# A hybrid decoder layer on one core: where the low parts of the operands are made, how the softmax sum and the head norm's root are formed, and how Strassen's input blocks are split

## The chip, the core and the metric

The kernel runs on one core of one Trainium2 chip. The core has TensorE (PE, matrix products; its weight loads are shown as PEld), VectorE (DVE), ScalarE (ACT), GpSimd (POOL) and the queues that start DMA transfers (SP, and the ACT queue). The metric is the device time of one execution in microseconds (us); lower is better. Times of several runs are given as their median.

## The reference, cut to what matters

One inference step of one layer (DEPTH = 1, D_MODEL = 1024). 2048 prompt tokens with 16 meta tokens in front, and 8 running sequences of 8 tokens each (64 sample tokens), go through

```
z = x @ w_in                                   # q, k, v, c, vm, o, gates
att = swa_attend(q, k, v)                      # 8 heads of 64, 2 KV heads, 128-token band, sinks, ALiBi
  p = exp(s - mx); p = p / (sum(p) + exp(sink - mx)); att = p @ v
h_m = mlstm_chunk(...)                         # 4 heads of 128, causal conv, gates, chunkwise form
y = concat([head_norm(att, g_attn), head_norm(sigmoid(o) * h_m, g_mlstm)])
  head_norm(h, g) = (h - mean) * rsqrt(var + 1e-5) * g          # per head
x1 = layer_norm(ALPHA * x + y @ w_out)
ffn = (silu(x1 @ w_gate) * (x1 @ w_up)) @ w_down                # d_ff = 2816
out = layer_norm(ALPHA * x1 + ffn)
```

All inputs and outputs are fp32. The attention's v is centred over each head before it is used, so the mean of `att` over a head is zero and its variance is the mean square.

## The kernel before

**Products.** Most products use operands in a reduced form of fp32 (`F32R`). Each fp32 operand is split into a high part (a cast, done by `hi_of`, on ACT nearly always) and a low part (source minus high part, `split`, line 144, on the engine `veng`). `mm3` (lines 147 to 149) then issues three matmuls: high x high, high x low, low x high.

**Stages.** (1) Projection of v, gates and o for all tokens in 17 tiles. (2) Projection of q, k and the conv path in five groups of 426 tokens; while it runs, chunks of attention and mLSTM are worked off in the background. (3) The FFN stage, in four groups of tokens (widths `W2` = 512, 512, 544, 544). Each group has an output projection (`out_proj`), the first layer norm (`ln1`), gate and up products by Strassen's scheme with seven products (`strassen`, P1 to P7, inputs B11, B21, B22 and the differences T1 to T4, each half a group wide), the down projection (`down`) and the second layer norm (`ln2`).

**Weights.** Each weight block (128 x 512) is loaded by the SP queue into `wr`, and `wblock` splits it: high part on ACT (line 135), low part on DVE, or on POOL where the block's number modulo 5 is 1 or 3 (`NPW`), two of five. Blocks are made `LOOK` = 5 ahead of their use. `sums` makes the sums of weights for Strassen's scheme on POOL early on and stores them in `SW`.

**Background.** `bg_attn(c)` is one 128-query chunk of attention and `bg_ml(c)` one of mLSTM; both are generators that are advanced one step at a time between the products (`pace`), and drained (`bg_drain`) where a group needs them. In `bg_attn`, the scores go to `P` (line 567), ACT takes the exponentials with their sums in `den` (line 575), DVE scales each head's `P` by 1/`den` (line 581), TensorE transposes (line 591) and multiplies by v (line 598). Then `att_rstd` (lines 516 to 531) forms the head norm: squares on ACT, split in two, a product with a constant block matrix `blk` that gives every element the mean square of its head (128 x 512), and on that whole width `rsqrt`: an integer start value and three Newton steps, nine wide operations (lines 158 to 160) behind lines 527, 153 and 155. The layer norms use a compact form, `spread_rstd`: per-token sums by matmuls with one column (line 499), the root on a few columns, and matmuls with the identity that spread it over the partitions again (line 511).

**Second layer norm.** `ln2` of a group runs as a generator `pend`, advanced in `after` behind the products P3 and P5 of the next group; while it is pending, the background is not advanced. Its squares are summed on POOL and DVE (line 1159).

**Order.** The functions are written out in the order of the products, but each engine's queue is ordered by a planner at build time, which simulates the kernel by estimated durations; a tile that waits for a free buffer waits in that order. The pools that matter here: `xpl` with 22 tiles (`x_tile`, for Y, the split input blocks and the first projection), `fp` with 7 `ft` tiles (`ftmp`), 6 `xx` tiles for the input blocks used last, 16 `z` tiles.

Of the kernel before, what the change touches and what calls it, by code (L numbers as in the profile page):

```python
# [17 lines left out]
KD = 8  # L18
# [33 lines left out]
NPW = (1, 3)  # L52
# [10 lines left out]
def tile_hymba(  # L63
# [47 lines left out]
    blk = cp.tile([128, 128], F32R, name="blk")  # L111
# [4 lines left out]
    def constants():  # L116
        SP.dma_start(out=C, in_=cst)
        SP.dma_start(out=Q, in_=par)
        SP.dma_start(out=R, in_=rows.to_broadcast([128, 16]))
        V.memset(avg, 1.0 / D)  # L120
        V.memset(one1, 1.0)
        V.tensor_copy(blk, C[:, C_BD:C_BD + 128])
# [393 lines left out]
    def att_rstd(o, w):  # L516

        sq = t2k("pt", [128, 512], PTB)
        A.activation(out=sq[:, 0:w], in_=o[:, 0:w], func=AF.Square)
        sh, sl = (t2k("pt", [128, 512], PTB, F32R) for _ in range(2))  # L520
        split("a", sh[:, 0:w], sl[:, 0:w], sq[:, 0:w])
        yield
        var = bps()
        PE.matmul(var[:, 0:w], lhsT=blk, rhs=sh[:, 0:w], start=True, stop=False)
        PE.matmul(var[:, 0:w], lhsT=blk, rhs=sl[:, 0:w], start=False, stop=True)
        ve = t2k("pt", [128, 512], PTB)
        V.tensor_scalar(out=ve[:, 0:w], in0=var[:, 0:w], scalar1=EPS, scalar2=None, op0=ALU.add)
        ry, tt = (t2k("pt", [128, 512], PTB) for _ in range(2))
        rsqrt(ve[:, 0:w], ry[:, 0:w], tt[:, 0:w])
        yield  # L530
        return ry

    def bg_attn(c):
# [45 lines left out]
        V.reciprocal(out=den, in_=den)  # L579
        for h in range(8):  # L580
            V.tensor_scalar(out=Pt[:, h, 0:nk], in0=Pt[:, h, 0:nk], scalar1=den[:, h:h + 1],
                            scalar2=None, op0=ALU.mult)
# [26 lines left out]
        rb = yield from att_rstd(o, 512)  # L609
# [129 lines left out]
    def bg_sample_attn():  # L739
# [64 lines left out]
        rb = yield from att_rstd(o, 256)  # L804
# [251 lines left out]
    with ExitStack() as s2:  # L1056
# [113 lines left out]
        def ln1(g, fast=False, marks={}):  # L1170


            z, w = P[g]["z"], WH[g]
            x = P[g]["x"] = {}
            for b in ("B11", "B21", "T2", "T1", "T3", "B22", "T4"):
                x[b] = []
                for k in range(4):
                    own = b == "T4" or b == "B22" and k > 1
                    x[b].append(fp.tile([128, FW], F32R, tag="xx", name="x", bufs=6) if own else x_tile())

            def hl(b, k, src, veng=V):
                t = x[b][k]
                return split("a", t[:, 0:w], t[:, HW:HW + w], src, veng)
# [8 lines left out]
            a, b = slice(0, w), slice(w, 2 * w)  # L1192
# [9 lines left out]
            t1, t2 = [], []  # L1202
            for k in range(4):
                t = ftmp()
                t1.append(t[:, 0:w])
                t2.append(t[:, HW:HW + w])
                G.tensor_tensor(out=t1[k], in0=z[k][:, b], in1=z[k][:, a], op=ALU.subtract)
                V.tensor_tensor(out=t2[k], in0=z[k + 4][:, b], in1=t1[k], op=ALU.subtract)
                hl("T2", k, t2[k])
                hl("T1", k, t1[k])  # L1210
                if k % 2:
                    yield
            for k in range(4):
                t = ftmp()
                t3, t4 = t[:, 0:w], t[:, HW:HW + w]
# [47 lines left out]
        def strassen(S, name):  # L1263
# [5 lines left out]
            def fn(wb):  # L1269
# [8 lines left out]
                x = [(t[:, 0:w], t[:, HW:HW + w]) for t in P[S["g"]]["x"][xs]]  # L1278
                product(p, wb, x, name in ("P1", "P2", "P5"), True, True)
# [16 lines left out]
                after(name)  # L1296
# [5 lines left out]
        def after(name):  # L1302
            if pend[0] is not None:
                if name in ("P3", "P5") and next(pend[0], 0) == 0:
# [76 lines left out]
        for g in range(NG):  # L1381
# [49 lines left out]
            else:  # L1431
# [13 lines left out]
                for m in range(KD):  # L1445
                    down(g, s, m, cc[1:], True, KD - 1, step(gen, 1))
# [129 lines left out]
```

## Time and profile before

| what | value |
|---|---|
| time before, median of 2 runs | 2691.45 us (2690.14 to 2692.76) |
| the profiled execution | 2694.93 us |
| its span, first to last instruction | 2693.1 us |
| mean granted TensorE clock | 0.954 |
| DMA | 409.29 MB, mean 152 GB/s |
| instructions | 44641 |

How to read the rows below: a group row gives line, engine, operation, output<-inputs, shapes and count, then the busy time in us and the mean duration of one in ns, then the idle time of the engine just before it and who ended that. Busy times of one engine can overlap in themselves, TensorE's above all, since its matmuls are pipelined. A waits row reads "who waited <- for whom: us in total, times, longest".

### The profile page before, as it was taken

Reading aid. Unit: us, or ns where it says so; the run is one execution under the profiler, and the core shown is the slowest. Engines: PE = TensorE matmul, PEld = TensorE weight load, DVE = VectorE, ACT = ScalarE, POOL = GpSimd, SP = SyncE. Lnnn points to the kernel's source line nnn. Section 1 sums busy time; section 2 is a strip of 40 time slices with the busy share of each in tenths; the row PEclk is TensorE's granted clock in tenths of the full one; section 3 lists DMA queues with packets and bytes.
Section 4 is the critical chain, followed back from the end, with each engine's and each line's share of the span. In section 5 each row is a group of like instructions: output and inputs, shape, how many; then the busy total and the mean of one; then the engine's idle time right before and its main releaser. Section 6 shows DMA issues by size and latency. Waiting matters only on the chain. (4 is left out here: it accounts for less than half of the span.)

```text
span 2693.1 us, 44641 instructions
## 1 busy us (share of the span) xinstructions
PE 2447.9 (91%) x16021; PEld 2234.5 (83%) x16021; DVE 1743.9 (65%) x3726; ACT 1183.3 (44%) x2598; POOL 914.7 (34%) x815
## 2 busy tenths in 40 slices
PE   9999889766999999988999989789999998899996
PEld 8999777655887888767888888688889997899996
DVE  5224365667677877677887785865775558755556
ACT  3113333444544555346454452452444535444453
POOL 3323333204322333363332233632222247322234
PEclk9999999868999999988999999799999998999997
DMA  8644766542554545425554553265444532444443
GB/s 295 221 137 162 241 210 220 174 142 80 163 151 151 158 154 156 150 63 190 165 154 142 159 167 99 59 202 145 128 137 142 170 94 88 140 137 141 137 149 105
DMA packets 302713, 409.29 MB, mean 152 GB/s; under 512 B 31442, under 2 KB 172842, under 8 KB 302474
## 3 DMA queue, kind: packets, MB, share of 16 engines
q1 hardware_dynamic: 260240, 351.54, 43.1%
q10 hardware_dynamic: 42250, 54.89, 5.6%
q8 instruction: 126, 2.06, 0.3%
q14 instruction: 97, 0.79, 0.1%
HBM read 339.26 MB, written 68.06 MB: 151 GB/s over the span
## 5 line engine op out<-in xcount | busy, mean ns | idle before, releaser
L147 PE MATMUL gps<-x,w 128*128 128x272 f32 (+3 forms) x2968 | 875.3, 302 | 68.0 <-ACT ft L1288 28.7
L135 ACT CAST w<-wr 128x512 fp32r<-128x512 f32 (+1 forms) x898 | 541.6, 611 | 839.1 <-PE gps L148 725.4
L144 POOL TENSOR_TENSOR w<-wr,w 128x512 fp32r<-128x512 f32 (+1 forms) x360 | 491.1, 1365 | 1200.7 <-ACT w L135 1101.8
L148 PE MATMUL gps<-x,w 128*128 128x272 f32 (+3 forms) x2968 | 879.8, 298 | 20.3 <-DVE x L144 20.2
L149 PE MATMUL gps<-x,w 128*128 128x272 f32 (+3 forms) x2968 | 866.8, 298 | 7.0 <-DVE w L144 5.5
L147 PEld LDWEIGHTS gps<-x,w 128*128 128x128 f32 x2968 | 564.8, 192 | 101.3 <-ACT ft L1288 31.3
L148 PEld LDWEIGHTS gps<-x,w 128*128 128x128 f32 x2968 | 571.4, 193 | 36.4 <-DVE x L144 26.4
L149 PEld LDWEIGHTS gps<-x,w 128*128 128x128 f32 x2968 | 565.7, 193 | 18.2 <-DVE w L144 6.3
L144 DVE TENSOR_TENSOR w<-wr,w 128x512 fp32r<-128x512 f32 (+1 forms) x538 | 423.6, 793 | 160.6 <-ACT w L135 136.7
L147 PE MATMUL gps<-h,w 128*128 128x272 f32 (+1 forms) x1056 | 351.3, 335 | 28.7 <-DVE z L1321 16.9
L148 PE MATMUL gps<-h,w 128*128 128x272 f32 (+1 forms) x1056 | 345.8, 328 | 4.2 <-DVE h L144 4.2
L149 PE MATMUL gps<-h,w 128*128 128x272 f32 (+1 forms) x1056 | 343.7, 327 | 1.0 <-DVE w L144 1.0
L147 PEld LDWEIGHTS gps<-h,w 128*128 128x128 f32 x1056 | 200.9, 191 | 54.9 <-DVE z L1321 25.5
L1321 DVE SCALAR_TENSOR_TENSOR z<-z,gps 128x272 f32<-128x272 f32 (+1 forms) x240 | 122.7, 516 | 149.7 <-PE gps L149 149.3
L148 PEld LDWEIGHTS gps<-h,w 128*128 128x128 f32 x1056 | 201.7, 191 | 19.8 <-DVE h L144 6.0
L149 PEld LDWEIGHTS gps<-h,w 128*128 128x128 f32 x1056 | 201.3, 191 | 18.3 <-DVE w L144 1.4
L198 POOL TENSOR_TENSOR st<-sa 128x256 f32<-128x256 f32 x88 | 67.7, 790 | 215.3 <-DMA SW<-st 180.6
L144 DVE TENSOR_TENSOR x<-x 128x426 fp32r<-128x426 f32 (+3 forms) x72 | 54.5, 757 | 103.1 <-ACT x L135 86.9
L1122 POOL TENSOR_TENSOR zs<-zs,z 128x512 f32<-128x512 f32 (+2 forms) x58 | 76.6, 1323 | 46.9 <-DVE z L1135 30.5
L135 ACT CAST x<-x 128x426 fp32r<-128x426 f32 (+3 forms) x72 | 42.0, 585 | 109.7 <-DMA x<-in_xT 55.5
L1254 DVE SCALAR_TENSOR_TENSOR ft<-ft 128x512 f32<-128x512 f32 (+1 forms) x88 | 76.6, 883 | 12.5 <-ACT ft L1253 12.0
L1257 DVE SCALAR_TENSOR_TENSOR ft<-ft 128x512 f32<-128x512 f32 (+1 forms) x88 | 79.6, 906 | 7.6 <-ACT ft L1294 6.1
(351 smaller groups left out, 3841.1 us busy)
## 6 DMA issues: line engine op xcount, KB each, us to landing
wr<-SW SPq DMA_DIRECT2D x352, 256.0 KB, 2.8
wr<-in_wd SPq DMA_DIRECT2D x168, 256.0 KB, 2.8
wr<-in_wg SPq DMA_DIRECT2D x132, 256.0 KB, 2.8
wr<-in_wu SPq DMA_DIRECT2D x132, 256.0 KB, 2.8
SW<-st ACTq DMA_DIRECT2D x44, 512.0 KB, 5.2
wr<-in_wo SPq DMA_DIRECT2D x64, 256.0 KB, 2.8
sa<-in_wg SPq DMA_DIRECT2D x22, 512.0 KB, 4.7
sa<-in_wu SPq DMA_DIRECT2D x22, 512.0 KB, 4.8
```

The source lines that it names most:

```text
L135: A.copy(out, src)
L144: return veng.tensor_tensor(out=lo, in0=src, in1=hi.bitcast(F32), op=ALU.subtract)
L147: PE.matmul(out, lhsT=wh, rhs=xh, start=start, stop=False, **kw)
L148: PE.matmul(out, lhsT=wh, rhs=xl, start=False, stop=False, **kw)
L149: PE.matmul(out, lhsT=wl, rhs=xh, start=False, stop=stop, **kw)
L198: G.tensor_tensor(out=t[:, i], in0=x, in1=y, op=op)
L1122: G.tensor_tensor(out=s[:, c], in0=s[:, c], in1=z[m][:, c], op=ALU.add)
L1254: V.scalar_tensor_tensor(out=c, in0=t, scalar=1.0, in1=c, op0=ALU.add, op1=ALU.mult)
L1257: V.scalar_tensor_tensor(out=c, in0=c, scalar=0.5, in1=P[g]["gate"].pop(2 * S["q"] + i), op0=ALU.mult, op1=ALU.mult)
L1321: V.scalar_tensor_tensor(out=zm, in0=zm, scalar=ALPHA if s == 0 else 1.0, in1=p, op0=ALU.mult, op1=ALU.add)
```

## The change

1. `NPW` becomes empty: the low part of every weight block is made on DVE.
2. `bg_attn` no longer scales `P` by 1/`den`. The unscaled product goes on, and `att_rstd` gets `den`: since the head norm divides by the root of variance + EPS, the unscaled variance is used with EPS x den x den.
3. `att_rstd` is compact: the squares are not split; four matmuls (two columns each) give the mean square per query and head, the root is taken on 8 columns (4 in the sample chunk), and eight matmuls with the identity spread it. The constant `blk` goes.
4. In `ln1` the differences for T1 and T3 are made on DVE, and the low parts of B22 and T4 too. Blocks are split two at a time into shared tiles: B21 with B22 (directly from z), T1 with T2, T3 with T4; B11 stays alone.
5. `after` advances the pending `ln2` only from the second round of products (q > 0) on.
6. In the last group, the first three of the last eight down items advance `ln2` by two steps, not one.

```diff
-NPW = (1, 3)
+NPW = ()
...
-    def att_rstd(o, w):
+    def att_rstd(o, nb, den=None):
+        w, k = 128 * nb, 2 * nb
         sq = t2k("pt", [128, 512], PTB)
         A.activation(out=sq[:, 0:w], in_=o[:, 0:w], func=AF.Square)
-        sh, sl = (t2k("pt", [128, 512], PTB, F32R) for _ in range(2))
-        split("a", sh[:, 0:w], sl[:, 0:w], sq[:, 0:w])
+        vp = bps()
+        for t in range(nb):
+            PE.matmul(vp[:, 0:k].rearrange("p (g t) -> p t g", g=2)[:, t, :], lhsT=sq[:, 128 * t:128 * t + 128],
+                      rhs=C[:, C_BD:C_BD + 128:64], start=True, stop=True)
+        t_ = t2k("rs", [128, 24], 2)
+        ve, ry, tt = t_[:, 0:k], t_[:, 8:8 + k], t_[:, 16:16 + k]
+        if den is None:
+            V.tensor_scalar(out=ve, in0=vp[:, 0:k], scalar1=EPS, scalar2=None, op0=ALU.add)
+        else:
+            V.scalar_tensor_tensor(out=tt, in0=den, scalar=EPS, in1=den, op0=ALU.mult, op1=ALU.mult)
+            V.tensor_tensor(out=ve, in0=tt, in1=vp[:, 0:k], op=ALU.add)
+        rsqrt(ve, ry, tt)
         yield
-        var = bps()
-        PE.matmul(var[:, 0:w], lhsT=blk, rhs=sh[:, 0:w], start=True, stop=False)
-        PE.matmul(var[:, 0:w], lhsT=blk, rhs=sl[:, 0:w], start=False, stop=True)
-        ve = t2k("pt", [128, 512], PTB)
-        V.tensor_scalar(out=ve[:, 0:w], in0=var[:, 0:w], scalar1=EPS, scalar2=None, op0=ALU.add)
-        ry, tt = (t2k("pt", [128, 512], PTB) for _ in range(2))
-        rsqrt(ve[:, 0:w], ry[:, 0:w], tt[:, 0:w])
-        yield
-        return ry
+        rb = bps()
+        for t in range(nb):
+            for g in range(2):
+                PE.matmul(rb[64 * g:64 * g + 64, 128 * t:128 * t + 128],
+                          lhsT=ry[:, nb * g + t:nb * g + t + 1].to_broadcast([128, 64]), rhs=ident,
+                          start=True, stop=True)
+        return rb
...
         V.tensor_tensor(out=den, in0=den, in1=es, op=ALU.add)
-        V.reciprocal(out=den, in_=den)
-        for h in range(8):
-            V.tensor_scalar(out=Pt[:, h, 0:nk], in0=Pt[:, h, 0:nk], scalar1=den[:, h:h + 1], ...)
...
-            for b in ("B11", "B21", "T2", "T1", "T3", "B22", "T4"):
-                    own = b == "T4" or b == "B22" and k > 1
+            x11 = [x_tile() for _ in range(4)]
+            for n in ("B", "T", "U"):
+                for d in (xh, xl):
+                    d[n] = [own() if n == "U" and (d is xl or k > 1) else x_tile() for k in range(4)]
...
+            def hl2(n, k, src, names, veng=V):
+                h, l = xh[n][k], xl[n][k]
+                for m, c in zip(names, (a, b)):
+                    x[m][k] = (h[:, c], l[:, c])
+                return split("a", h[:, 0:2 * w], l[:, 0:2 * w], src, veng)
...
-                hl("B11", k, z[k][:, a])
-                marks[7] = hl("B21", k, z[k + 4][:, a]).ins
+                hl1(k, z[k][:, a])
+                marks[7] = hl2("B", k, z[k + 4][:, 0:2 * w], ("B21", "B22")).ins
...
-                G.tensor_tensor(out=t1[k], in0=z[k][:, b], in1=z[k][:, a], op=ALU.subtract)
-                V.tensor_tensor(out=t2[k], in0=z[k + 4][:, b], in1=t1[k], op=ALU.subtract)
-                hl("T2", k, t2[k])
-                hl("T1", k, t1[k])
+                V.tensor_tensor(out=t[:, a], in0=z[k][:, b], in1=z[k][:, a], op=ALU.subtract)
+                V.tensor_tensor(out=t[:, b], in0=z[k + 4][:, b], in1=t[:, a], op=ALU.subtract)
+                hl2("T", k, t[:, 0:2 * w], ("T1", "T2"))
...
-                G.tensor_tensor(out=t3, in0=z[k + 4][:, b], in1=z[k][:, b], op=ALU.subtract)
-                V.tensor_tensor(out=t4, in0=z[k + 4][:, a], in1=t2[k], op=ALU.subtract)
-                hl("T3", k, t3)
-                hl("B22", k, z[k + 4][:, b], G)
-                hl("T4", k, t4, G)
+                V.tensor_tensor(out=t[:, a], in0=z[k + 4][:, b], in1=z[k][:, b], op=ALU.subtract)
+                V.tensor_tensor(out=t[:, b], in0=z[k + 4][:, a], in1=ts[k][:, b], op=ALU.subtract)
+                hl2("U", k, t[:, 0:2 * w], ("T3", "T4"))
...
-                if name in ("P3", "P5") and next(pend[0], 0) == 0:
+                if S["q"] and name in ("P3", "P5") and next(pend[0], 0) == 0:
...
-                    down(g, s, m, cc[1:], True, KD - 1, step(gen, 1))
+                    down(g, s, m, cc[1:], True, KD - 1, step(gen, 2 if m < 3 else 1))
```

More of the change, by code (lines that the diff above doesn't have):

```diff
@@ L110, in tile_hymba @@
     avg = cp.tile([128, 128], F32, name="avg")
-    blk = cp.tile([128, 128], F32R, name="blk")
     ident = C[:, C_ID:C_ID + 128]
@@ L121, in constants @@
         V.memset(one1, 1.0)
-        V.tensor_copy(blk, C[:, C_BD:C_BD + 128])
     NC4 = (NCH + 1) * 4
@@ L578, in bg_attn @@
         V.tensor_tensor(out=den, in0=den, in1=es, op=ALU.add)
-        V.reciprocal(out=den, in_=den)
-        for h in range(8):
-            V.tensor_scalar(out=Pt[:, h, 0:nk], in0=Pt[:, h, 0:nk], scalar1=den[:, h:h + 1],
-                            scalar2=None, op0=ALU.mult)
         yield
@@ L608, in bg_attn @@
                          scale=Q[:, Q_GA + t:Q_GA + t + 1])
-        rb = yield from att_rstd(o, 512)
+        rb = yield from att_rstd(o, 4, den)
         ysf = ys.rearrange("p t q -> p (t q)")
@@ L803, in bg_sample_attn @@
                 yield
-        rb = yield from att_rstd(o, 256)
+        rb = yield from att_rstd(o, 2)
         ys = t2k("ys", [128, 4, 128], 2)
@@ L1173, in ln1, with own, hl1 @@
             z, w = P[g]["z"], WH[g]
-            x = P[g]["x"] = {}
-            for b in ("B11", "B21", "T2", "T1", "T3", "B22", "T4"):
-                x[b] = []
-                for k in range(4):
-                    own = b == "T4" or b == "B22" and k > 1
[L1179 to L1183, printed above, removed]
+            a, b = slice(0, w), slice(w, 2 * w)
+            x = P[g]["x"] = {n: [None] * 4 for n in ("B11", "B21", "B22", "T1", "T2", "T3", "T4")}
+            def own():
+                return fp.tile([128, FW], F32R, tag="xx", name="x", bufs=6)
+            x11 = [x_tile() for _ in range(4)]
+            xh, xl = {}, {}
+            for n in ("B", "T", "U"):
+                for d in (xh, xl):
+                    d[n] = [own() if n == "U" and (d is xl or k > 1) else x_tile() for k in range(4)]
+            def hl1(k, src):
+                t = x11[k]
+                x["B11"][k] = (t[:, 0:w], t[:, HW:HW + w])
+                return split("a", t[:, 0:w], t[:, HW:HW + w], src)
+            def hl2(n, k, src, names, veng=V):
[3 more added lines that the diff above has]
+                return split("a", h[:, 0:2 * w], l[:, 0:2 * w], src, veng)
             cc = [slice(o, o + n) for o, n in cols(W2[g])]
@@ L1191, in ln1 @@
                     yield
-            a, b = slice(0, w), slice(w, 2 * w)
             for k in range(4):
@@ L1197, in ln1 @@
                                  bias=Q[:, Q_L1B + kk:Q_L1B + kk + 1])
-                hl("B11", k, z[k][:, a])
-                marks[7] = hl("B21", k, z[k + 4][:, a]).ins
+                hl1(k, z[k][:, a])
+                marks[7] = hl2("B", k, z[k + 4][:, 0:2 * w], ("B21", "B22")).ins
                 if k % 2:
                     yield
-            t1, t2 = [], []
+            ts = []
             for k in range(4):
                 t = ftmp()
-                t1.append(t[:, 0:w])
-                t2.append(t[:, HW:HW + w])
-                G.tensor_tensor(out=t1[k], in0=z[k][:, b], in1=z[k][:, a], op=ALU.subtract)
-                V.tensor_tensor(out=t2[k], in0=z[k + 4][:, b], in1=t1[k], op=ALU.subtract)
-                hl("T2", k, t2[k])
-                hl("T1", k, t1[k])
+                ts.append(t)
+                V.tensor_tensor(out=t[:, a], in0=z[k][:, b], in1=z[k][:, a], op=ALU.subtract)
+                V.tensor_tensor(out=t[:, b], in0=z[k + 4][:, b], in1=t[:, a], op=ALU.subtract)
+                hl2("T", k, t[:, 0:2 * w], ("T1", "T2"))
                 if k % 2:
@@ L1277, in fn @@
                 p = S["be" if name == "P2" else "ga" if name in ("P5", "P3") else "al"][:, a]
-                x = [(t[:, 0:w], t[:, HW:HW + w]) for t in P[S["g"]]["x"][xs]]
-                product(p, wb, x, name in ("P1", "P2", "P5"), True, True)
+                product(p, wb, P[S["g"]]["x"][xs], name in ("P1", "P2", "P5"), True, True)
                 c1, c2 = S["c"]
@@ L1295, in fn, with after @@
                     gated(S, 1)
-                after(name)
+                after(S, name)
             item(fn, (wsrc(S["mt"], S["q"], ws), 4))
         pend, rate = [None], [0.0]
-        def after(name):
+        def after(S, name):
             if pend[0] is not None:
-                if name in ("P3", "P5") and next(pend[0], 0) == 0:
+                if S["q"] and name in ("P3", "P5") and next(pend[0], 0) == 0:
                     pend[0] = None
```

1 line of the change is left out of this document (removed).

## The prediction

> **What bounds the kernel now.** I read the shares of the engines first, then the windows by stage, then TensorE's waits, and last the single operations that stand in those waits. In a windows row the columns are the stretch, its length, then busy time and (count) for PE, PEld, DVE, ACT and POOL, the granted TensorE clock, the DMA share and GB/s.
>
> ```profile
> PE 2447.9 (91%) x16021; PEld 2234.5 (83%) x16021; DVE 1743.9 (65%) x3726; ACT 1183.3 (44%) x2598; POOL 914.7 (34%) x815
> ...
> 505.00:577.00 72.00, 37.48 (x163) 26.35 (x161) 50.90 (x171) 25.53 (x67) 3.27 (x3) 0.71 0.40 119
> 660.00:677.00 17.00, 0.62 (x3) 0.33 (x2) 16.34 (x28) 13.11 (x35) 9.16 (x12) 0.50 0.00 0
> ...
> 700.00:1100.00 400.00, 376.97 (x2617) 336.37 (x2616) 316.70 (x712) 207.06 (x482) 114.36 (x83) 0.99 0.51 156
> 1250.00:1690.00 440.00, 419.58 (x2870) 374.16 (x2870) 334.21 (x714) 215.34 (x495) 135.00 (x100) 0.99 0.51 155
> ...
> 1229.00:1237.00 8.00, 0.43 (x4) 0.22 (x3) 3.75 (x4) 3.48 (x7) 7.76 (x6) 0.65 0.41 131
> 1760.00:1769.00 9.00, 0.69 (x4) 0.51 (x3) 5.83 (x5) 5.02 (x10) 8.74 (x6) 0.72 0.41 127
> 2287.00:2293.00 6.00, 1.50 (x12) 1.28 (x11) 4.74 (x5) 2.80 (x7) 5.76 (x6) 1.00 0.61 182
> 2360.00:2400.00 40.00, 40.00 (x322) 40.00 (x321) 24.27 (x38) 22.28 (x44) 14.47 (x11) 1.00 0.60 174
> ```
>
> TensorE bounds it. Where nothing disturbs it (2360 to 2400) it starts 322 matmuls in 40 us, one every 0.124 us, at full clock; these matmuls stay. What a change on DVE or POOL can give is the time in which TensorE does not stream. That time sits in few places: 505 to 577 holds 163 matmuls in 72 us, 660 to 677 only three, and the starts of the three later token groups (1229, 1760, 2287) hold 4, 4 and 12 matmuls in 8, 9 and 6 us. Against the page's 9% of idle TensorE, the Trainium skill ("Trainium Kernel Development and Optimization", Performance Expectations) says that matmul busy time is a bad measure because matmuls overlap, and that the share of weight loads is better. By that the room would be 17% and not 9%; the counts above agree with it in kind, and the terms below are taken from single stretches, so neither share enters them.
>
> Who ends TensorE's waits, first in the stretch 500 to 620, then over the FFN (680 to 2640); columns are total us, times, longest:
>
> ```profile
> PE gps L989 <- DVE cz L981: 13.4, 2, 8.1
> PE bps L646 <- DVE qs L641: 10.8, 1, 10.8
> PE bps L591 <- DVE P L581: 7.0, 1, 7.0
> ...
> PE gps L147 <- ACT ft L1288: 28.7, 10, 8.3
> PE gps L148 <- DVE x L144: 19.3, 13, 3.0
> PE gps L147 <- DVE z L1321: 17.2, 28, 1.8
> ...
> PE gps L149 <- DVE w L144: 6.5, 4, 3.3
> ```
>
> In the first stretch the last to arrive is DVE, three times. In the FFN the longest sum is an eviction on ACT (L1288); the low parts of the weights are hardly waited for (6.5 us on DVE).
>
> **Roots and softmax, in the drained stretch.** From 505 to 577 two chunks of attention and mLSTM are run out before the output projection can start, with little else for TensorE. DVE's groups in that window (busy us, mean ns):
>
> ```profile
> L160 DVE SCALAR_TENSOR_TENSOR pt<-pt 128x512 f32<-128x512 f32 x6 | 4.1, 686 | 0.0
> L158 DVE TENSOR_TENSOR pt<-pt 128x512 f32<-128x512 f32 x6 | 4.1, 684 | 0.0
> L159 DVE SCALAR_TENSOR_TENSOR pt<-pt 128x512 f32<-128x512 f32 x6 | 4.1, 683 | 0.0
> ...
> L581 DVE TENSOR_SCALAR P<-P,mx 128x256 f32<-128x256 f32 x8 | 2.2, 349 | 0.0
> ...
> L527 DVE TENSOR_SCALAR pt<-bps 128x512 f32<-128x512 f32 x2 | 1.4, 688 | 0.1
> ...
> L160 DVE SCALAR_TENSOR_TENSOR dn<-dn 128x4 f32<-128x4 f32 x6 | 1.0, 162 | 0.2
> ```
>
> The wide root is 18 operations of 0.68 us, 12.3 us, with L527 1.4 and L153 and L155 about 1.6 (four of half that length, from the same list): 15.3 us for two chunks. The compact root has 13 operations a chunk on 8 columns instead of 512; at the 0.162 us of the 4-column row that is 4.2 us. Gone also: the eight scalings (2.2 us here) and the low part of the squares (0.69 each, as a 512-wide operation). DVE saves 15.3 - 4.2 + 2.2 + 1.4 = 14.7 us. DVE is what TensorE waits for there, with L641 and L591 behind these operations in its queue, so nearly all is on the path. I take **-15**. Bounds: 0, if ACT's exponentials and the DMAs of the next chunk end the waits instead; -25, if the clock (0.71 here) also comes back for the 37 us of matmuls.
>
> The other 14 chunks lie beside dense matmuls and save DVE time, not path: there L591 waited for L581 only a little, so I take -2, between 0 and -10. TensorE pays for the compact form:
>
> ```profile
> L511 PE MATMUL bps<-C,rs x48: 223/275/482, 1249.9 to 2685.0; 68*128 68x68 f32 x32, 128*128 128x128 f32 x16
> L524 PE MATMUL bps<-pt,blk x17: 278/397/792, 341.1 to 1991.9; 128*128 128x512 f32 x16, 128*128 128x256 f32 x1
> ...
> 2664.62 0.79 PE bps L499 x8
> 2667.77 1.99 PE bps L511 x8
> ```
>
> Eight L511 take 1.99 us and eight L499 0.79 us (4 of them 0.4), so the new 8 + 4 cost about 2.4 us; the two 512-wide matmuls that go are 2 x 0.397 = 0.8. That is +1.6 a chunk at most, and +0.5 if the 64-row halves run side by side. Eleven chunks and the sample chunk lie in the FFN, where every TensorE microsecond counts: +6 to +19, I take **+10**. The planner that orders each queue can place these small matmuls inside products, as it now does with others, so the wait for the squares on ACT needs not stop TensorE.
>
> **Low parts of the weights.** Duration minimum/median/maximum, and a pair in the stall at 1229:
>
> ```profile
> L135 ACT CAST w<-wr x898: 390/621/667, 492.9 to 2656.2; 128x512 fp32r<-128x512 f32 x173, 128x256 fp32r<-128x256 f32 x7
> L144 DVE TENSOR_TENSOR w<-wr,w x538: 412/691/1844, 494.1 to 2656.2; 128x512 fp32r<-128x512 f32 x172, 128x256 fp32r<-128x256 f32 x8
> L144 POOL TENSOR_TENSOR w<-wr,w x360: 732/1294/2218, 493.6 to 2659.5; 128x512 fp32r<-128x512 f32 x173, 128x256 fp32r<-128x256 f32 x7
> ...
> 1230.29 1.71 POOL L144 TENSOR_TENSOR w<-wr,w 128x512 fp32r<-128x512 f32 x1
> 1231.97 5.74 POOL L1159 TENSOR_TENSOR ft<-ft 128x512 f32<-128x512 f32 x4
> ...
> 1230.80 1.75 DVE L144 TENSOR_TENSOR w<-wr,w 128x512 fp32r<-128x512 f32 x1
> ...
> 1236.40 0.37 ACT L1288 COPY ft<-gps 128x256 f32<-128x256 f32 x1 [0.71 <-POOL ft L1159]
> ```
>
> 360 operations move to DVE at the median 0.69 us: +248 us of DVE work. Against it: scalings, wide roots and the low part of the squares go (7.65 + 2.2 + 0.7 - 2.1, about 8.5 us a chunk by the window's rows, some 135 us), and DVE's operations that read two tensors of SBUF are stretched while POOL runs: the same 512-wide subtraction has a median of 0.69, but 1.75 beside POOL's. The mean of that group over the run is 424/538 = 0.79, so 0.1 x 538 = 54 us of stretching in this one group; POOL's weight work is 491 of 915 us, so about half of it goes, and as much again in the other two-input groups. I put DVE's total at 1744 + 248 - 135 - 60 = about 1800 us, 67%: no relief in the mean, but no more 1.7 us operations in front of evictions.
>
> At the starts of the groups this is on the path. At 1230 POOL runs a weight's low part between the sums of squares (L1159) of the second layer norm; ACT's squares wait for their buffers, the eviction L1288 stands behind them on ACT and waits for L1159 too, and TensorE waits for the bank. The change takes the weights off POOL and lets the second layer norm's steps begin one round of products later. Of 23 us in the three stretches 20 matmuls need 2.5, so 20.5 are lost; POOL's own L1159 stay, at 1.3 to 1.4 us. I take **-14**, between 0 and -20.
>
> Between these places the waits of the FFN list without L1288 (19.3, 17.2, 6.5 and smaller ones) are partly such stretched operations in front of an eviction or a split. I take **-20**; bounds -45, and +45 for the case in which DVE gets the bound (below).
>
> **Input blocks.** L1207 and L1216, 32 subtractions, and the low parts of B22 and T4 go from POOL to DVE, and splits are made two at a time.
>
> ```profile
> L144 DVE TENSOR_TENSOR x<-ft,x x48: 410/432/1501, 675.0 to 2269.5; 128x256 fp32r<-128x256 f32 x24, 128x272 fp32r<-128x272 f32 x24
> ...
> x<-YD SPq DMA_DIRECT2D x16, 256.0 KB, 4.2
> ```
>
> Per group DVE gets 8 subtractions (0.43) and one half of 8 joined splits more, about 5 us, and loses POOL's stretching; ACT issues 16 casts instead of 28. In the first layer norm at 660, where DVE is busy 16.3 of 17 us, I see no gain above 2. The joined tiles cost something else: B21 and B22 now share a tile, so it comes free after the last P3 and not after P2, and the next group's Y loads, which take 24 tiles of a pool of 22, wait for it. A load lands after 4.2 us and is split in 1.3; P4 and the first half of the projection, 1.5 and 1.5 to 3 us, cover about 4 of these 5.5. Three times 1.5 is 5 us. Together **+2**, between -8 and +15. **The end:** two steps of the layer norm instead of one in three of the last items: **-2**, between +2 and -6.
>
> **Sum:** -15 - 2 + 10 - 14 - 20 + 2 - 2 = -41 us. The profiled execution took 2694.93 with a span of 2693.1; the median shown is 2691.45, 3.5 us less. The forecast is 2691.45 - 41 = **2650 us**, 1.5% faster. A measurement of this kernel tells about 2%, 54 us, from no change.
>
> **Rivals.** *DVE becomes the bound* (slower). For: DVE is busy 79% from 700 to 1100 and 76% from 1250 to 1690, and a Strassen product of about 1.45 us gets a whole 0.69 us split on DVE instead of three of five. If none of the stretching goes, 1250 to 1690 gains some 75 blocks x 0.69 = 52 us against about 3 chunks x 8.5 = 25 us saved: 361 of 440, 82%, locally full where a chunk and the gating fall together. Should TensorE wait 5% of three such stretches of 400 us, that is +60 and gives about 2710. It decides from a DVE share of about 90% in these windows. Against: part of today's 79% is stretching itself, and in the quiet stretch at 2360 a DVE at 61% (24.27 of 40) never stops TensorE. *The stretching is the whole story*: every eviction in the FFN comes early, the interior gives -45, the starts -20, the drained stretch -25 with its clock: -41 - 25 - 6 - 10 = -82, 2609 us. The rows on 505 to 577 (0.71) and 660 to 677 (0.50) carry the clock part: 37.48 x 0.29 is 11 us. The Trainium skill ("TensorE: Matmul & The Clock Gate", Part 1) has the clock halve after an idle window of some 3.4 us and return after as long a busy one; the rows agree that long idle stretches come with a lower clock, and by the rule this part would come with any stall that falls under that length. *The change moves work that was hidden anyway*: POOL's remaining operations still stretch DVE's, the Y loads are late, and only the roots count: -15 + 10 + 5 = 0, 2691 us.
>
> **Chances.** Forecast (-20 to -65) 0.50; stretching the whole story (-65 to -100) 0.17; hidden anyway (-20 to +10) 0.21; DVE the bound (+10 to +70) 0.12. Leaving out a tenth at each end gives 2600 to 2700. Faster by over 2% is the second case and a third of the first, 0.34; slower by over 2% a third of the last, 0.04; within 0.62.
>
> **What will show it.** Roots: no wide root on DVE, 505 to 577 shorter by 10 to 20 us, L646's wait of 10.8 about halved. POOL: no weights, DVE's weight split at a mean near 0.69, and DVE's busy share between 64% and 72%. Starts of groups: no wait of TensorE for L1288 over 4 us. Input blocks: TensorE's waits for Y splits at the output projections, 0 to 5 us each. I am wrong if TensorE's waits for DVE evictions or weight splits grow beyond 50 us in the FFN (DVE the bound), or if the interior's waits vanish altogether.

## The result, and the profile after

| | before | after |
|---|---|---|
| median of 2 runs | 2691.45 us | 2621.16 us (2620.30 to 2622.01) |
| span of the profiled execution | 2693.1 us | 2619.6 us |
| mean granted TensorE clock | 0.954 | 0.970 |

The ratio is 0.9739 (95% interval 0.9697 to 0.9781): 70 us less, 2.6%. The forecast was 2650; the time lies inside the range, but in the case that the prediction called the second (-65 to -100), not in its own.

The shares of the engines after. Columns: busy us, share of the span, instructions.

```profile
PE 2445.0 (93%) x16383; PEld 2234.3 (85%) x16383; DVE 1688.2 (64%) x3956; ACT 1171.4 (45%) x2533; POOL 365.1 (14%) x391
```

POOL lost 550 us. DVE took over 360 weight splits, and is busy 56 us *less* than before.

The stages after, in the windows view with the columns of the prediction's first fence. The rows answer, in order, to the drained stretch, the first layer norm, the two long stretches of products, the starts of the second, third and fourth group, and a quiet stretch.

```profile
505.00:562.00 57.00, 40.94 (x194) 27.59 (x191) 31.39 (x123) 23.04 (x63) 1.71 (x2) 0.73 0.33 101
645.00:662.00 17.00, 1.20 (x6) 0.90 (x5) 16.09 (x34) 13.17 (x25) 0.00 (x0) 0.50 0.00 0
700.00:1100.00 400.00, 396.13 (x2768) 351.76 (x2766) 290.54 (x756) 211.88 (x499) 11.06 (x10) 1.00 0.53 160
1250.00:1690.00 440.00, 422.09 (x2922) 377.52 (x2920) 323.02 (x804) 212.61 (x480) 39.11 (x32) 0.97 0.49 148
1221.00:1229.00 8.00, 2.53 (x16) 2.33 (x15) 6.77 (x6) 4.50 (x9) 7.61 (x6) 0.76 0.43 111
1726.00:1734.00 8.00, 3.19 (x19) 2.98 (x18) 6.77 (x6) 4.22 (x9) 7.61 (x6) 0.78 0.44 125
2266.00:2270.00 4.00, 1.87 (x14) 1.66 (x14) 3.15 (x10) 0.93 (x2) 0.00 (x0) 0.96 0.49 168
2290.00:2330.00 40.00, 40.00 (x324) 39.78 (x323) 30.80 (x65) 27.53 (x58) 5.57 (x7) 1.00 0.58 174
```

There is a gain where no hole was: from 700 to 1100 TensorE starts 2768 matmuls in the 400 us that held 2617, and its busy time goes from 377 to 396. Not all of that is saved, because the FFN stage now begins 16 us earlier, the compact roots bring small matmuls, and background work has moved. Taken from the first P1 eviction of a group to that of the next (in the last group to its last down eviction), the four groups took 504, 536, 526 and 398 us before and take 499, 506, 515 and 391 after, so 30 of the 53 us lie in the second. The first layer norm is as long as it was. The holes at the starts hold 16, 19 and 14 matmuls instead of 4, 4 and 12: smaller, but there. In the quiet stretch nothing changed (324 in 40 us), and DVE, now at 77% there, does not stop TensorE.

TensorE's waits after in the window 680 to 2640, which the prediction used for the FFN, and below the line of dots the start of the prediction's first stretch (500 to 620). Columns: total us, times, longest. L1298 is the eviction of P7 (L1288 before), L1331 the eviction of the down projection (L1321), L142 and L133 the low and high parts (L144, L135).

```profile
PE gps L145 <- ACT x L133: 19.6, 8, 5.5
PE gps L145 <- ACT ft L1298: 19.4, 13, 5.5
PE gps L145 <- DVE z L1331: 13.9, 27, 2.1
PE bps L497 <- POOL ft L1164: 7.6, 1, 7.6
PE gps L146 <- DVE x L142: 5.7, 4, 2.0
...
PE bps L651 <- DVE qs L646: 6.1, 2, 5.9
PE bps L522 <- ACT pt L519: 3.0, 2, 1.7
```

All rows of this view for that window add up to 134 us in 124 waits before and 99 us in 89 after; those that DVE ended went from 72 to 39. The window is not the same work in both kernels: after, the last down eviction comes at 2593.5, and the row L497 above and a few others belong to the last layer norm behind it. Between the first P1 eviction and the last down eviction, which is called the FFN stage from here on, the waits went from 135 us to 87. In the drained stretch the wait for L646 went from 10.8 to 6.1 us; of the 13.4 us for L981 (now L986) 1.3 are left, and the 7.0 us for L581 are gone. New are 3.0 us for the squares on ACT and 2.6 for the exponentials.

The clock went with the stalls. These are the first three rounds of products of the third group, before and then after; the granted clock is the third number from the end:

```profile
1739.10:1868.50 129.40, 112.56 (x770) 101.72 (x770) 73.26 (x153) 51.66 (x101) 50.97 (x38) 0.93 0.53 160
```
```profile
1687.70:1795.60 107.90, 97.06 (x707) 90.25 (x706) 72.07 (x139) 49.95 (x98) 15.50 (x11) 0.97 0.58 175
```

63 of the matmuls moved to other places, so not all of the 21.5 us by which the stretch got shorter is saved (a run below shortens such stretches and saves nothing); its clock went from 0.93 to 0.97.

### The profile page after: what moved, and what is told of

It is laid out like the page before. It is cut to its first block, busy times and chain, and to the rows that moved or that the text cites. A ratio compares the mean times of both kernels' runs of the same rounds, so it can differ in the third digit from the quotient of the medians.

```text
span 2619.6 us, 44985 instructions
## 1 busy us (share of the span) xinstructions
PE 2445.0 (93%) x16383; PEld 2234.3 (85%) x16383; DVE 1688.2 (64%) x3956; ACT 1171.4 (45%) x2533; POOL 365.1 (14%) x391
## 4 chain that ended last, share of the span: by engine, by line
PE 45%; DVE 4%; DMA 3%; ACT 2%; issue 1%; POOL 1%; ACTq 0%; SPq 0%; DVEq 0%; POOLq 0%
PE gps L145 14%; PE gps L146 13%; PE gps L147 13%; DVE z L1172 1%; PE bps L571 1%; DMA P<-GW 1%; DMA x<-YD 1%; DVE w L142 1%; ACT w L133 1%; DVE z L1331 1%; DVE z L1157 0%; POOL ft L1164 0%; DMA out_oS<-P 0%; PE bps L596 0%; DMA z<-in_xT 0%
## 5 line engine op out<-in xcount | busy, mean ns | idle before, releaser
L133 ACT CAST w<-wr 128x512 fp32r<-128x512 f32 (+1 forms) x898 | 543.6, 611 | 842.3 <-PE gps L146 746.6
L142 DVE TENSOR_TENSOR w<-wr,w 128x512 fp32r<-128x512 f32 (+1 forms) x898 | 634.9, 714 | 217.9 <-ACT w L133 189.7
L1331 DVE SCALAR_TENSOR_TENSOR z<-z,gps 128x272 f32<-128x272 f32 (+1 forms) x240 | 123.1, 518 | 146.4 <-PE gps L147 145.7
L142 DVE TENSOR_TENSOR x<-x 128x426 fp32r<-128x426 f32 (+3 forms) x72 | 51.6, 717 | 121.8 <-ACT x L133 102.2
L703 POOL TENSOR_SCALAR_AFFINE_SELECT P<-P 128x512 f32<-128x512 f32 x16 | 15.7, 979 | 808.3 <-DMA P<-GW 709.4
L1127 POOL TENSOR_TENSOR zs<-zs,z 128x512 f32<-128x512 f32 (+2 forms) x58 | 83.5, 1441 | 128.5 <-DVE z L1140 57.5
L1164 POOL TENSOR_TENSOR ft<-ft 128x272 f32<-128x272 f32 (+1 forms) x56 | 60.7, 1083 | 254.2 <-ACT ft L1159 201.6
L133 ACT CAST x<-x 128x426 fp32r<-128x426 f32 (+3 forms) x72 | 42.1, 585 | 107.6 <-DMA x<-in_xT 59.1
L1125 POOL TENSOR_TENSOR zs<-z 128x512 f32<-128x512 f32 (+2 forms) x10 | 13.1, 1314 | 498.5 <-DVE z L1331 258.4
```

The lines of the kernel that those rows point to most:

```text
L133: A.copy(out, src)
L142: return veng.tensor_tensor(out=lo, in0=src, in1=hi.bitcast(F32), op=ALU.subtract)
L703: G.affine_select(out=gm, in_=gm, pattern=[[0, 4], [1, 128]], compare_op=ALU.is_ge, fill=BIG, base=0, channel_multiplier=-1)
L1127: G.tensor_tensor(out=s[:, c], in0=s[:, c], in1=z[m][:, c], op=ALU.add)
L1164: (V if len(qs) > 1 else G).tensor_tensor(out=q, in0=q, in1=t[:, 0:w], op=ALU.add)
L1331: V.scalar_tensor_tensor(out=zm, in0=zm, scalar=ALPHA if s == 0 else 1.0, in1=p, op0=ALU.mult, op1=ALU.add)
```

## The experiments

Twelve kernels, in three groups. Their names begin with u where a part of the change is undone, with o where one part, or two, stands alone in the kernel before, and with p where the changed kernel is probed. "The guard" is the condition q > 0 of part 5. Changes in us are 2691.45 x (1 - ratio), so that kernels from different chips can be set side by side. The intervals are about 0.2% each way, some 5 us, but that of the change itself is 0.4%, some 11 us, so a difference to the change of less than about 10 us is not told from none.

| kernel | ratio to before (95%) | us |
|---|---|---|
| the change | 0.9739 (0.9697 to 0.9781) | -70 |
| change without the weights' part (u_npw) | 0.9853 (0.9822 to 0.9884) | -40 |
| change without the later layer norm (u_q) | 0.9800 (0.9778 to 0.9823) | -54 |
| change without roots and softmax (u_roots) | 0.9767 (0.9747 to 0.9787) | -63 |
| change without the input blocks (u_x) | 0.9771 (0.9752 to 0.9789) | -62 |
| weights alone (o_npw) | 0.9790 (0.9770 to 0.9811) | -57 |
| roots and softmax alone (o_roots) | 0.9827 (0.9807 to 0.9848) | -47 |
| later layer norm alone (o_q) | 1.0003 (0.9991 to 1.0014) | 0 |
| weights and later layer norm (o_npw_q) | 0.9747 (0.9732 to 0.9763) | -68 |
| change, POOL's load given back as dead work (p_dummy) | 1.0125 (1.0100 to 1.0151) | +34 |
| u_npw with the norms' sums on DVE (u_npw_sumv) | 0.9791 (0.9768 to 0.9814) | -56 |
| change with the norms' sums on DVE (p_sumv) | 0.9732 (0.9711 to 0.9754) | -72 |
| change with eight `ft` buffers (p_ftb8) | 0.9757 (0.9740 to 0.9775) | -65 |

### One part taken back

**Weights.**

```diff
-NPW = ()
+NPW = (1, 3)
```

> The changed kernel, with two of five weight blocks split on POOL again (NPW = (1, 3)). Theory A (POOL's weight splits stand in front of the second layer norm's sums and stretch DVE's operations; taking them away is the gain at the starts of the groups): slower than the changed kernel by 30 to 50 us, 2650 to 2670, and the stretch from the first to the fourth round of products of groups 1 and 2 is longer by 10 to 20 us each. Theory B (it is the later start of the second layer norm that frees the starts): slower by no more than 12 us, 2622 to 2633, and those stretches grow by under 5 us each.

31 us of the 70 go: theory A's size. The first three rounds of the second and third group are 8.1 and 14.2 us longer than in the change, where theory A had 10 to 20.

**Later layer norm.**

```diff
-                if S["q"] and name in ("P3", "P5") and next(pend[0], 0) == 0:
+                if name in ("P3", "P5") and next(pend[0], 0) == 0:
```

> The changed kernel, with the pending second layer norm advanced from the first round of products again. Theory A: within 8 us of the changed kernel, 2615 to 2630. Theory B: slower by 25 to 45 us, 2645 to 2665, with TensorE's waits for L1298-like evictions of over 4 us at the starts of groups 1 to 3.

16 us: between the two theories, so neither the guard nor the weights carry the starts alone. The longest waits for P7 at the second and third start are 7.5 and 4.8 us, against 5.5 and 4.8 in the change.

**Roots and softmax**: `att_rstd`, its calls, the scalings of `P` and `blk` go back.

```diff
+        V.reciprocal(out=den, in_=den)
+        for h in range(8):
+            V.tensor_scalar(out=Pt[:, h, 0:nk], in0=Pt[:, h, 0:nk], scalar1=den[:, h:h + 1],
+                            scalar2=None, op0=ALU.mult)
...
-        rb = yield from att_rstd(o, 4, den)
+        rb = yield from att_rstd(o, 512)
```

> The changed kernel, with the wide root, the split squares, the block matrix and the scaling of P by 1/den as before. My sum: the output projection of group 0 starts 12 to 16 us later, and TensorE's small matmuls (10 us) are saved in the FFN, so +3 to +8 us, 2624 to 2629. Rival (DVE's time in the FFN counts too, since the weights are on it now): +20 to +35 us, 2641 to 2656.

8 us, with intervals that overlap. The drained stretch behaves as the prediction had it: the first eviction of the output projection comes at 599.0 us after, 612.3 with the wide roots, 611.2 before.

**Input blocks**: `ln1` and the tiles that it takes go back.

```diff
-                V.tensor_tensor(out=t[:, a], in0=z[k + 4][:, b], in1=z[k][:, b], op=ALU.subtract)
-                hl2("U", k, t[:, 0:2 * w], ("T3", "T4"))
+                G.tensor_tensor(out=t3, in0=z[k + 4][:, b], in1=z[k][:, b], op=ALU.subtract)
+                hl("T3", k, t3)
+                hl("B22", k, z[k + 4][:, b], G)
+                hl("T4", k, t4, G)
```

> The changed kernel, with the input blocks split one at a time and the differences T1, T3 and the low parts of B22, T4 on POOL as before. My sum: within 5 us, 2616 to 2626. Rival (POOL's operations at the starts of groups stretch DVE's and hold the first products): +10 to +25 us, 2631 to 2646, most of it before the first product's eviction of each group.

9 us, between the two, and again the intervals overlap. The four costs sum to 64 of 70, which looks as if the parts simply added. They do not, as the third group shows.

### What POOL's load costs

**POOL's old load as dead work.** The products use DVE's low parts; POOL makes the same ones a second time.

```diff
-            split("a", hi[:, 0:n], lo[:, 0:n], raw[:, 0:n], G if wcount[0] % 5 in NPW else V)
+            split("a", hi[:, 0:n], lo[:, 0:n], raw[:, 0:n])
+            if wcount[0] % 5 in (1, 3):
+                G.tensor_tensor(out=spare[:, 0:n], in0=raw[:, 0:n], in1=hi[:, 0:n].bitcast(F32), op=ALU.subtract)
```

> The changed kernel, to which POOL's old load is given back as dead work: for two of five weight blocks POOL makes the low part a second time into a tile that nobody reads; the product uses DVE's. So POOL is as busy as before the change and raw and high tiles are held as long, but no product waits for POOL's low part. Theory A (POOL's presence costs: it stretches DVE's two-input operations and its queue delays the sums of squares of the layer norms): at least 20 of the 31 us that undoing the weights cost come back, so +20 to +45 us against the changed kernel, some 2650 to 2670; a DVE weight split goes from 0.71 us in the mean to 0.79 or more. Theory B (POOL's own slow low parts came late, and the products waited for them): within 10 us of the changed kernel, under 2637.

104 us more than the change, over twice theory A's upper end, and 34 above the kernel before. Theory B falls: no product waits for POOL's result here. Nor is it the tiles that POOL's dead work holds for longer: TensorE's waits for high and low parts of weights come to 3.8 and 1.4 us. Its engines:

```profile
PE 2483.7 (91%) x16383; PEld 2257.2 (83%) x16383; DVE 1910.0 (70%) x3956; ACT 1169.1 (43%) x2533; POOL 925.4 (34%) x751
```

DVE executes the same 3956 instructions as in the change and needs 1910.0 us for them instead of 1688.2: 560 us of POOL cost DVE 222 us. The groups of DVE in the FFN show on which operations. Weight split and gating in this kernel, then in the change:

```profile
L142 DVE TENSOR_TENSOR w<-wr,w 128x512 fp32r<-128x512 f32 x809 | 700.3, 875 | 137.7 <-ACT w L133 122.5 <-issue 2.6 <-PE gps L146 2.2
L1268 DVE SCALAR_TENSOR_TENSOR ft<-ft 128x544 f32<-128x544 f32 x42 | 41.4, 1002 | 0.9 <-ACT ft L1267 0.8
...
L1304 DVE TENSOR_TENSOR ft<-ft,gps 128x272 f32<-128x272 f32 x42 | 18.1, 431 | 6.4 <-PE gps L147 6.2
```
```profile
L142 DVE TENSOR_TENSOR w<-wr,w 128x512 fp32r<-128x512 f32 x826 | 589.5, 720 | 197.2 <-ACT w L133 169.2 <-PE gps L146 5.4 <-issue 4.9
L1268 DVE SCALAR_TENSOR_TENSOR ft<-ft 128x544 f32<-128x544 f32 x44 | 31.7, 721 | 0.7
...
L1301 DVE TENSOR_TENSOR ft<-ft,gps 128x272 f32<-128x272 f32 x44 | 19.2, 436 | 16.2 <-PE gps L147 16.0
```

The split goes from 720 to 875 ns, the gating of two SBUF tensors from 721 to 1002, while the addition that takes one input from PSUM stays at 0.43 us (L1304 here is L1301 there). And TensorE waits for what stands behind them:

```profile
PE gps L145 <- ACT ft L1301: 34.5, 16, 9.3
PE gps L145 <- DVE z L1334: 25.6, 33, 3.4
PE gps L146 <- DVE x L142: 13.7, 15, 4.2
```

These are the evictions of P7 and of the down projection and a split of x: 34.5, 25.6 and 13.7 us against 19.4, 13.9 and 5.7 in the change. This kernel is close to the prediction's rival *DVE becomes the bound*, built: all low parts on DVE and the stretching not gone. It was priced at 2710; 1.0125 x 2691.45 is 2725.

**POOL's weights, without a layer norm behind them.** Besides `NPW = (1, 3)`:

```diff
-                    (V if len(qs) > 1 else G).tensor_tensor(out=q, in0=q, in1=t[:, 0:w], op=ALU.add)
+                    V.tensor_tensor(out=q, in0=q, in1=t[:, 0:w], op=ALU.add)
```

> The changed kernel with the low parts of two of five weight blocks back on POOL (which alone cost 31 us), but with the sums of squares of the layer norms all on DVE, so that no layer norm stands behind a weight in POOL's queue. Theory Q (the cost sits in POOL's queue, in front of the sums of squares, at the starts of the groups): 15 us or more of the 31 go, so a ratio below 0.980 and TensorE's waits for the eviction P7 under 4 us at each start. Theory S (the cost is the stretching of DVE's operations and late low parts all over the products): within 8 us of the kernel with POOL's weights, ratio 0.982 to 0.988, and the first three rounds of each group stay some 8 us longer than in the changed kernel.

17 of the 31 us come back. The P7 waits at the starts of the second and third group, with the sums on POOL and then on DVE:

```profile
PE gps L145 <- ACT ft L1298: 9.1, 2, 8.2
PE gps L145 <- ACT ft L1298: 8.7, 3, 7.2
```
```profile
PE gps L145 <- ACT ft L1298: 5.0, 2, 4.4
PE gps L145 <- ACT ft L1298: 4.1, 3, 2.9
```

Theory Q has the size right (15 us or more), though only about 9 of the 17 us show in these waits and the longest is 4.4, not under 4. The first three rounds are 0.9 us shorter than in the change in the second group and 8.0 longer in the third, which fits Q once and S once. The run does not separate the two causes by itself: moving the 56 additions also takes 69 us of work off POOL (854.5 to 785.3), and DVE needs only 23 us more for them (1599.6 to 1622.9) where 56 x 0.7 us would be 39, so some stretching went with them.

**The same edit in the changed kernel.**

> The changed kernel with the sums of squares of the layer norms on DVE and not on POOL (about 100 additions of 0.7 us on DVE for 1.3 on POOL). If POOL's sums are what still delays the starts (waits of 5.5 and 4.8 us for the eviction P7): -5 to -12 us. If they are hidden, or DVE's queue takes their place in the delay: within 4 us.

2 us, inside the interval; it is 56 additions by the instruction counts, not some 100. Here the same move takes 67 us of work off POOL and DVE needs only 7 us more, so as much or more stretching goes as beside POOL's weights, and nothing is gained. That speaks for the place in POOL's queue as the main part of the 17 us above, and for the stretching in the other 14, without showing the split. The waits for P7 at the second and third start fall from 6.3 and 6.0 to 3.8 and 3.5 us, and the time does not follow.

### One part alone

**Weights alone** (`NPW = ()` in the kernel before).

> The kernel before with one part of the change alone: all low parts of the weights on DVE; the wide roots and the scalings of P stay on DVE, so DVE gets 360 operations more and loses none. If the parts are independent: -25 to -35 us, as undoing this part cost 31. If DVE is the bound without the relief by the roots (the rival of the prediction): no gain, 0 to +40 us, with DVE above 85% busy in the stretches with attention chunks. In between, -5 to -20, both are at work.

57 us: more than any theory gave, and nearly twice what undoing it cost. DVE:

```profile
PE 2433.6 (92%) x16021; PEld 2225.7 (84%) x16021; DVE 1809.0 (69%) x4086; ACT 1183.0 (45%) x2598; POOL 428.5 (16%) x455
```

360 operations more, 65 us more. At 0.69 us they would be 248; so by this estimate 183 us of stretching left DVE's operations. Counted another way, the time of DVE's operations above the median of their own line and shape is 221 us in all before and 73 here, 148 less.

**Weights and later layer norm** (both one-line edits in the kernel before).

> The kernel before with two parts: all low parts of the weights on DVE, and the second layer norm held back to the second round of products. The weights alone gave 57 us when added to the kernel before, but undoing them in the changed kernel cost only 31. Theory O (the parts overlap: both take the layer norm's sums out of the delay at the starts, POOL's queue being the common cause): the guard adds little to the weights, 0 to 6 us, 2634 to 2641. Theory I (the parts are independent, and the guard gives its 16 us here too): about 2624, and then the compact roots and the joined blocks together are worth nothing in the end.

-68 us, 11 of them from the guard, between theory O and theory I. These two small edits give all that the change gives but 2 us, which is less than the intervals can tell.

**Roots and softmax alone** (parts 2 and 3 in the kernel before).

> The kernel before with the compact roots and the folded softmax sum alone. By the prediction's terms: -15 in the drained stretch, -2 elsewhere, +10 for TensorE's small matmuls, -7 in all, 2690; undoing them in the changed kernel cost 8. If the relief of DVE counts where POOL still stretches its operations (the DVE is fuller in this kernel): -20 to -30, and the first three rounds of the second and third group shorten by 4 us or more each. If the small matmuls weigh more: 0 to +8.

-47 us. The prediction's terms gave -7; undoing it cost 8. So what the roots are worth depends on POOL. The first three rounds of the second and third group are 6.5 and 15.0 us shorter than before. The engines:

```profile
PE 2454.1 (93%) x16383; PEld 2241.7 (85%) x16383; DVE 1599.5 (61%) x3580; ACT 1177.5 (45%) x2581; POOL 901.7 (34%) x815
```

The FFN stage, in the windows view, for before, roots alone, weights alone, weights with later layer norm, and the change:

```profile
698.80:2662.90 1964.10, 1828.10 (x12885) 1684.40 (x12883) 1372.02 (x2815) 935.45 (x2042) 690.15 (x536) 0.97 0.46 141
```
```profile
686.80:2612.10 1925.30, 1828.89 (x13159) 1692.45 (x13157) 1268.99 (x2716) 933.02 (x2030) 679.21 (x536) 0.97 0.48 144
```
```profile
699.50:2612.00 1912.50, 1814.76 (x12900) 1678.10 (x12898) 1438.72 (x3165) 935.14 (x2042) 225.96 (x191) 0.98 0.50 145
```
```profile
697.70:2604.70 1907.00, 1808.86 (x12902) 1675.81 (x12900) 1444.03 (x3166) 937.73 (x2042) 222.42 (x191) 0.98 0.49 145
```
```profile
682.70:2593.50 1910.80, 1823.73 (x13168) 1687.45 (x13166) 1357.50 (x3078) 928.70 (x1994) 175.82 (x143) 0.98 0.48 145
```

The second number is the length: 1964, 1925, 1912, 1907, 1911. Roots alone take 39 us off, by giving DVE 103 us less to do; the weights take 52 off, with DVE 67 us *fuller*; together they take no more than the weights with the guard. In the same stage, TensorE's waits and the time for which the trace has its clock at half:

| kernel | length | waits | at half clock |
|---|---|---|---|
| before | 1964 | 135 | 113 |
| roots alone | 1925 | 96 | 99 |
| weights alone | 1912 | 97 | 89 |
| weights and later layer norm | 1907 | 98 | 82 |
| the change | 1911 | 87 | 72 |
| POOL's load as dead work | 2001 | 145 | 126 |

The waits fall to nearly the same by either part alone. The two parts seem to remove largely the same waits in different ways: fewer operations in DVE's queue, or faster ones. Waits plus half of the time at half clock is an estimate of what TensorE loses; it overcounts where TensorE waits at half clock. Against the kernel before, it falls by 50 and 53 us in the two kernels with wide roots, whose stage got 52 and 57 us shorter. In the three kernels with compact roots the stage stays behind the estimate: 39 us shorter for 46, 53 for 69, and 37 longer for 17 in the last. These 7 to 20 us are of the size of the +6 to +19 that the prediction put on the small matmuls, though no run shows those alone. What the roots still give beside the weights is the start: the FFN stage begins 15 us earlier (682.7 against 697.7), and runs 4 us longer, with its 266 matmuls more.

**Later layer norm alone** (part 5 in the kernel before).

> The kernel before with the second layer norm held back to the second round of products, alone. POOL still makes two of five weight blocks. If POOL's queue in front of the sums of squares is what delays the starts, this alone gives most of what moving the sums to DVE gave beside POOL's weights (17 us): -12 to -22 us, TensorE's waits for the eviction P7 under 4 us at the starts. If the delay only moves one round later with the layer norm: -5 to +4 us.

Nothing (1.0003), the expectation's second case. The first three rounds of the second and third group are 10 and 9 us shorter than before, but hold 47 and 44 matmuls fewer: the work moved and nothing was saved. A likely reason, which no run shows directly, is that POOL makes weights in every round, so that sums held back by one round stand behind other weights. The waits for P7 at the second and fourth start went from 8.1 and 7.2 us to 6.2 and 7.8; at the third it was 9.4 before, and here, in the same stretch of the run:

```profile
PE gps L147 <- ACT ft L1288: 11.5, 3, 7.2
```

**Eight `ft` buffers in the changed kernel.**

```diff
-FTB = 7
+FTB = 8
```

> The changed kernel with eight instead of seven buffers for the tiles that evictions, squares and gating share. If the remaining waits for the eviction P7 at the starts (5.5 and 4.8 us) and for an eviction of the first stage's late tiles (15.8 us) come from that pool being empty: -8 to -20 us. If the next thing in the same queues ends the waits: within 5 us.

Not faster (0.9757 against 0.9739, the intervals overlap). P7's waits fall from 19.4 to 14.2 us, and the wait for the eviction L939 of the first stage is 15.5 us after 15.8; the time does not follow. No version that beats the change beyond its interval was found.

## Why the prediction was right and wrong

The direction and the limiting engine were right, and the sum of -41 us was 29 short. That the time still lies inside the range is owed to the range's width, not to the sum.

- **What bounds the kernel** held: TensorE, through the time in which it does not stream. The FFN stage got 53 us shorter, and TensorE's waits in it went from 135 to 87 us, 48 less. The time at half clock went from 113 to 72 us, worth up to 20 us more, and the small matmuls take some back; no experiment separates these.
- **Drained stretch, -15**: right. The output projection's first eviction comes 12.3 us earlier, P1's first 16.1, and without the roots nothing and 1.7 us are left of these gains.
- **Other chunks, -2, and small matmuls, +10**: right only beside a quiet POOL. In the FFN the compact form changed the stage by -39 us with POOL busy, and by nothing with the weights already off it (1911 us with the wide roots put back into the change, 1911 in the change). The error of the step is that L581 and the wide roots were held to be hidden, because TensorE seldom waited for *them* (1.6 us for L581 in the whole FFN stage); as we read it, it waited for evictions and splits that stood behind them in DVE's queue.
- **Weights: -14 at the starts and -20 between**: this is the term of the sum that was mis-sized. Put into the kernel before, the weights and the guard gave -68 in place of -34; taken out of the change one by one they cost 31 and 16. At the starts only part of it is seen: the longest P7 waits are 5.5 and 4.8 us, where none over 4 was forecast, and the sums for them on POOL are still there. Over the three starts the waits for P7 went from 24.7 to 16.1 us. That is 9 of the 48 us of waits that went; the larger part lies between the starts, where the prediction had put 20 and a bound of 45.
- **The step that failed** behind that size is DVE's total: 1744 + 248 - 135 - 60 = about 1800, measured 1688. The -135 for roots and scalings was good: roots alone take DVE from 1743.9 to 1599.5, 144 less, and putting them into the otherwise finished change takes 122 (1810.5 to 1688.2). The 60 was not: removing POOL's weights alone takes about 150 to 183 us of stretching away, by the two counts above. The prediction took the 60 from the mean of one group, 0.79 against a median of 0.69, halved it for POOL's other work and doubled it for "the other two-input groups". One-input operations are stretched too:

```profile
L581 DVE TENSOR_SCALAR P<-P,mx 128x256 f32<-128x256 f32 x88 | 44.9, 578 | 0.1
```
```profile
L581 DVE TENSOR_SCALAR P<-P,mx 128x256 f32<-128x256 f32 x88 | 24.1, 347 | 0.0
```

  Before and with the weights alone: 578 and 347 ns for the same 88 scalings. The second value stood in the prediction's own fence for the drained stretch (349); the same group over the whole FFN stage of the kernel before would have shown the first. The Trainium skill ("SBUF — State Buffer", Who interferes with whom) has this: DVE operations with two SBUF inputs, and also copies and tensor-scalar operations in a two-port mode, contend with GpSimd for a shared port pair. The rows agree in both kinds, and in the unaffected 0.43 us of the additions that read PSUM. That the scalings run in a two-port mode is not recorded; their time with the weights off POOL fits it, 284 ns at 144 columns and 347 at 256, or 0.56 ns a column, where the tensor-scalar operation that reads PSUM (L527) takes 424 ns at 256 and 682 at 512, 1.0 a column.
- **Input blocks, +2**: undoing them cost 9 us, at the edge of the lower bound of -8. Taken with the weights and the guard but without the roots they seem to cost 5; neither is clear of the intervals, and the sign stays open. The forecast waits for splits of Y and x are there: the row for L133 (L135 before) went from 12.9 to 19.6 us, the longest is 5.5, and without the input blocks the row has 14.0.
- **The end, -2**: from the last down eviction to the last operation of the layer norm 26.0 us before and 22.3 after, -3.7. It was not tried alone.
- **DVE the bound** (0.12): not what happened, but the mechanism is real, and p_dummy shows its price. Its deciding point, a share of about 90% from 700 to 1100 and from 1250 to 1690, was wrong: in p_dummy DVE is at 83% and 80% there and at 79% of the FFN stage (1571.92 of 2000.80), and the kernel loses 104 us; with the weights alone DVE is at 75% of the stage and the kernel gains 57. This points to the length of the operations ahead of an eviction, more than to the share; no run varies the one without the other.

```profile
688.80:2689.60 2000.80, 1855.59 (x13158) 1706.88 (x13156) 1571.92 (x3075) 926.77 (x1994) 711.81 (x485) 0.97 0.47 138
```

- **The stretching is the whole story** (0.17, 2609): nearest to the time, 12 us off where the forecast is 29. Its -45 for the interior was of the right order; its clock part for the drained stretch did not come (0.71 before, 0.73 after).
- **Hidden anyway** (0.21, 2691): no. It would have had undoing the weights cost nothing; it cost 31 us.

## What to carry to other kernels

Before moving work between DVE and GpSimd, list DVE's operations by shape with minimum, median and mean: where the mean lies above the median in several groups, the excess over all of them is a first estimate of what GpSimd's work costs DVE, and it can exceed what GpSimd saves. In this kernel it was 221 us before, 73 after the change, and 303 with POOL's load as dead work. Terms of a sum that relieve the same queue are not independent: roots and weights gave 47 and 57 alone and at most 70 together with two more parts; undoing parts one by one hides that, doing each alone shows it. A stretch that gets shorter is no saving until the work that left it is found: the later layer norm alone took 10 and 9 us off two starts and nothing off the time. An operation that nobody waits for can still count when the one behind it in its queue is an eviction: the roots alone took 39 us off the FFN stage, where hardly anyone waited for them.

## What was not expected of the hardware

DVE lost 222 us to 560 us of work on POOL, 0.4 us for each, with the same 3956 instructions. The stretch is in operations between SBUF tiles, one-input ones among them (the scalings, 347 ns with the weights off POOL and 578 before); additions with an input from PSUM stay at 0.43 us. Not every one-input operation is stretched: the statistics operation BATCH_NORM_STATS2 takes 0.28 us in the mean in the change and beside the dead work alike. And a part that gives nothing alone (the later layer norm, 1.0003) gives 11 to 16 us once POOL's queue is free.
